# Zeros for the query tiles in eight pieces behind the gates, and two later times in the scheduler of a two-layer hybrid decoder trunk

## The chip, the cores and the metric

The kernel runs on one core of one Trainium2 chip. The metric is the device time of one execution in microseconds (us), as the median of a few runs. One execution was also recorded by the hardware profiler; its rows are given in microseconds from the start of its span. TensorE is called PE here, VectorE DVE, ScalarE ACT, GpSimd POOL, and SyncE, which issues the DMAs, SP.

## The reference, cut to what matters

A sequence of 512 tokens with 1024 features passes through two layers. Each layer is a mixer and a feed-forward part:

```
h = rmsnorm(x);  proj = h @ w_in                       # 1024 -> 3592 columns
aq, ak, av = split(silu(causal_dwconv(a_qkv)))         # 4 heads x 128: gated DeltaNet
beta = sigmoid(a_b);  g = -exp(a_log) * softplus(a_a + dt_bias)
o_a = rmsnorm(gated_delta_rule(l2norm(aq), l2norm(ak), av, g, beta)) * silu(a_z)
o_b = dilated_attention(rope(b_q), rope(b_k), b_v)     # 8 heads x 64
x = x + rmsnorm(concat(o_a, o_b) @ w_out)
u = causal_dwconv(rmsnorm(x) @ ffn_up) + bias
x = x + rmsnorm((gelu(u_gate) * u_val) @ ffn_down)     # 2816 wide
```

The delta rule needs, per chunk, the decay between any two tokens, exp of a difference of cumulative sums of `g`. The dilated attention multiplies roped queries and keys of 64 features per head.

## The kernel before, in words

Activations lie with features on the 128 partitions and the 512 tokens along the free axis. A projection adds up products of 128x128 weight pieces with 128x512 activations in PSUM. Single precision is kept by splitting each operand into a high part in fp32r and a remainder: a row of a projection is three matmuls of 512 columns (high by high twice with the two activation parts, and the remainder of the weights once). In the trace it is a pair of lines, `psg<-hx,whi` x2 and `psg<-hx,wlo` x1. Weights arrive in units of 128x1024 (`raw`, line 250, from SP). ACT writes the high part `whi` (helper `act`, line 147), and DVE or POOL subtracts for the remainder `wlo` (helper `tt`, line 151): DVE as one instruction of 128x1024, POOL as four of 128x256. Which of the two takes a unit is decided when the program is built.

That decision, and the order of all instructions on all engines, comes from a small simulator inside the kernel, `_Sched`. Every stage is a generator. It issues some instructions, adds their modelled cost to a clock of its engine (`sc.op`), and yields the time at which it wants to go on; `sc.get` and `sc.put` model a buffer and the time it comes free, `sc.set` and `sc.wait` a flag. The generator with the best priority that is due goes next. So a yielded time does not delay anything on the chip: it only changes which instruction is written ahead of which, and which engine looks least loaded. On the chip each engine runs its list in order and waits for the data.

PSUM has eight banks: four of kind `g` for projections, three of kind `s`, and one of kind `o`. That single `o` bank serves, one after the other, the norm's sums, the gates and the four decay pieces.

The places that matter here, in the order of the mixer's start:

- The set-up of a layer. The four 128x1024 pieces of `x` are written to memory (`xspill`, line 737), and line 754 sets to zero the halves of two query tiles that stay unused: `qz[0]`, which shares the buffer of `bT[0]` and is called `bT` in the trace, and `qz[1]`, called `qz`. Each is one POOL instruction of 64 partitions by 2048. The simulator's clock for POOL does not count them.
- `gates()`: a chain of small DVE and ACT steps from the projected `dn_ab` to `dn_g`, then a matmul on PE into the `o` bank for the cumulative sums (in the trace `pso<-dn_g,cc`), then `dn_gc`, `dn_kds`, `dn_eg`, and the flag `eg`.
- `conv`: each projected head is scaled out of PSUM on DVE (`A<-psg,rs`) and convolved, one first tap on ACT and three on DVE (`kT<-A,vv,kT`, then `vb<-A,vv,vb`), 128 partitions by about 510 columns each.
- `decays()`: for each of four chunks, four matmuls into the `o` bank (`pso<-cc,dn_g`, recorded as x8), then DVE subtracts (`edec<-pso,dn_gc`), which frees the bank, then two ACT steps. I call the four chunks decay 0 to 3.
- `k_head`: PE transposes a key head (`pss<-cc,kT`), DVE forms `dn_dk` and `kd`.
- `inverse()` and `doubles`: from a memory round trip come `cpt` pieces, which PE multiplies in small matmuls of 16 columns (`pss<-cpt,xiT`, `pss<-C,xi`).
- The end of the mixer: attention's output is added into `bT` (`bT<-pso,bT`), gates multiply the delta rule's output (`vb<-vb,dn_rq`, `zt<-zt,vb`), and both are split for the output projection (`hx<-bT`, `hx<-zt`).

The roped queries are written into the used halves of `qz` by ACT, 64 partitions at a time, behind the query projection.

```
ps = yield from pget("o")            # decays(): the one o bank
r = tt(e[:, c], v4(ps), bc(gc[:, c]), ALU.subtract)
pput("o", r)                         # modelled as free when edec is done
```

Of the kernel before, what the change touches and what calls it, by code (L numbers as in the profile page):

```python
# [18 lines left out]
P = 128  # L19
# [5 lines left out]
NC = S // P  # L25
AH = 8
DH = 64
# [86 lines left out]
def kernel(ctx: ExitStack, tc: tile.TileContext, xT, w_ab, w_cm, w_tm, w_o, w_up, w_dn,  # L114
                      vec, rowc, cst, lnm, out):
    nc = tc.nc
# [12 lines left out]
    sc = _Sched()  # L129
# [20 lines left out]
    def tt(out_, a, b, op, after=0.0, eng="dve"):  # L150
        (nc.vector if eng == "dve" else nc.gpsimd).tensor_tensor(out_, a, b, op=op)  # L151
        n = out_.free_size()
        return sc.op(eng, 0.07 + n * 1.05e-3 if eng == "dve" else 0.18 + n * 2.07e-3, after)
# [18 lines left out]
    def vcopy(out_, a, after=0.0):  # L172
        nc.vector.tensor_copy(out_, a)
        return sc.op("dve", 0.07 + out_.free_size() * 1.0e-3, after)
# [12 lines left out]
    def wget(tag, cols=512):  # L187
        yield from sc.get(tag, BUFS[tag])
        return work(tag, cols)
# [4 lines left out]
    def pget(tag):  # L194
        yield from sc.get("ps" + tag, PB[tag])
        return psum(tag)

    def pput(tag, at):
        sc.put("ps" + tag, at)
# [4 lines left out]
    def bc(ap, n=P):  # L204
        return ap.unsqueeze(2).to_broadcast(list(ap.shape) + [n])
# [504 lines left out]
    def mixer(l, key, hx, acc2, rs, segs):  # L710
# [28 lines left out]
        def small(name, cols=4):  # L739
            return kp.tile([P, 4, cols], F32, tag="dn_" + name, bufs=1, name="dn_" + name)  # L740
# [9 lines left out]
        bT = [sp.tile([P, 4, S], F32, tag=f"s{8 + i}", name=f"bT{i}") for i in range(2)]  # L750
        bv = sp.tile([P, 4, S], F32, tag="s10", name="bv")
        qz = [bT[0], sp.tile([P, 4, S], F32, tag="qz", name="qz")]
        for i in range(2):
            nc.gpsimd.memset(qz[i][DH * (1 - i):DH * (2 - i)], 0.0)
        beta, g, t1, t2, t3, gc, eg, kds, dc, beg, rq, dk, br2, vsc = (small(x) for x in (
            "beta", "g", "t1", "t2", "t3", "gc", "eg", "kds", "dc", "beg", "rq", "dk", "br2", "vsc"))
        ea = kp.tile([P, 4], F32, tag="dn_ea", bufs=1, name="dn_ea")
# [3 lines left out]
        def K(*a):  # L761
            return (l,) + a
# [3 lines left out]
        def gates():  # L766
            ps = yield from pget("o")
            abr = yield from wget("C")
            r = vcopy(abr[0:16], pab[0:16])
            pput("g", r)  # L770
            yield r
            for c in range(NC):
                sc.t += 0.1
                pe.transpose(ps[:, c * 16:(c + 1) * 16], abr[0:16, c * P:(c + 1) * P], ident[0:16, 0:16])
            pv = ps[:, 0:64].rearrange("p (c k) -> p c k", c=4)
            vcopy(ab, pv[:, :, 8:16])
            r = tt(ab, pv[:, :, 0:8], ab, ALU.add)
            pput("o", r)
            sc.put("C", r)
            yield from sc.wait(*ready)  # L780
            r = tt(ab, ab, bc(rt, 8), ALU.mult)
            b, a = ab[:, :, 0:4], ab[:, :, 4:8]
            tables(T_EXP)
            act(ea, rc[:, 0:4], AF.Exp)
            rb = act(beta, b, AF.Exp, scale=-1.0, after=r)
            tt(g, a, rc[:, 4:8].unsqueeze(1).to_broadcast([P, 4, 4]), ALU.add)
            r = stt(t1, g, -1.0, g, ALU.mult, ALU.min)
            r = act(t1, t1, AF.Exp, after=r)
            yield r
            ts(beta, beta, 1.0, None, ALU.add, after=rb)  # L790
            recip(beta, beta)
            ts(t2, t1, 2.0, None, ALU.add)
            recip(t2, t2)
            tt(t1, t1, t2, ALU.mult)
            tt(t2, t1, t1, ALU.mult)
            r = ts(t3, t2, 1.0 / 15, None, ALU.mult)
            for k in (13, 11, 9, 7, 5, 3):
                r = stt(t3, t3, 1.0 / k, t2, ALU.add, ALU.mult, after=r)
            stt(t3, t3, 1.0, t1, ALU.add, ALU.mult)
            ts(g, g, 0.0, None, ALU.max)  # L800
            stt(g, t3, 2.0, g, ALU.mult, ALU.add)
            r = stt(g, g, -1.0, ea.unsqueeze(1).to_broadcast([P, 4, 4]), ALU.mult, ALU.mult)
            yield r + 2.0
            ps = yield from pget("o")
            gf = g.rearrange("p a b -> p (a b)")
            mm(ps[:, 0:16], utri, gf, True, True)
            mm(ps[:, 16:32], one.to_broadcast([P, P]), gf, True, True)
            yield sc.t + 0.15
            last = ps[:, 16:32].rearrange("p (a b) -> p a b", a=4)
            act(dc, last, AF.Exp)  # L810
            vcopy(gc, ps[:, 0:16].rearrange("p (a b) -> p a b", a=4))
            r = tt(kds, last, gc, ALU.subtract)
            pput("o", r)
            yield r
            act(kds, kds, AF.Exp)
            r = act(eg, gc, AF.Exp, after=r)
            sc.set(K("eg"), r)

        def decays():
            for c in range(NC):  # L820
                ps = yield from pget("o")
                for h in range(NH):
                    mm(ps[:, h * P:(h + 1) * P], g[:, c, h:h + 1].to_broadcast([P, P]), utri, True, True)
                yield sc.t + 0.15
                r = tt(e[:, c], v4(ps), bc(gc[:, c]), ALU.subtract)
                pput("o", r)
                yield r
                act(e[:, c], e[:, c], AF.Abs)
                r = act(e[:, c], e[:, c], AF.Exp, scale=-1.0)
                yield  # L830
            sc.set(K("gates"), r)
# [363 lines left out]
        def rope(i, c, ps):  # L1195
            yield from sc.wait(*ready)
            t = yield from wget("AB"[c // 2])
            r = act(t, ps, AF.Identity, scale=rt[:, c:c + 1])
            pput("g", r)
            yield r  # L1200
            sq = yield from sc.get("sq", 2)
            rab = kp.tile([P, 2, AH, 16], F32, tag="sq", bufs=2, name="rab")
            ra, rb = rab[:, 0], rab[:, 1]
            tv = t.rearrange("p (h d) -> p h d", h=AH)

            def tab(tb, lo, hi):
                return tb[:, c, lo:hi].unsqueeze(1).to_broadcast([P, AH, hi - lo])

            tt(ra, tv[:, :, 0:16], tab(cosr, 0, 16), ALU.mult)
            tt(rb[:, :, 0:8], tv[:, :, 8:16], tab(sinr, 0, 8), ALU.mult)  # L1210
            tt(rb[:, :, 8:16], tv[:, :, 0:8], tab(sinr, 8, 16), ALU.mult)
            r = tt(tv[:, :, 0:16], ra, rb, ALU.add)
            sc.put("sq", r)
            yield r
            pt = yield from pget("s")
            transposes(pt, [t[:, p * P:(p + 1) * P] for p in range(4)])
            sc.put("AB"[c // 2], sc.t)
            if i == 0:

                for j in range(2):  # L1220
                    bs = slice(DH * j, DH * (j + 1))
                    r = act(qz[j][bs, :, c * P:(c + 1) * P], v4(pt)[bs], AF.Copy, scale=DH ** -0.5)
            else:
                r = act(bT[i][:, :, c * P:(c + 1) * P], v4(pt), AF.Copy)
            pput("s", r)
            sc.set(K("b", i, c), r)
# [380 lines left out]
```

## Time and profile before

| what | value |
| --- | --- |
| median of 3 runs | 1411.35 us (1409.8 to 1412.21) |
| the profiled execution's own time | 1409.27 us |
| its span, first to last instruction | 1407.5 us |
| mean granted clock of PE in it | 0.989 |
| PE busy | 1365.3 us, 97% of the span, 7176 matmuls and transposes |
| DVE busy | 863.5 us, 61% |
| POOL busy | 706.7 us, 50% |
| ACT busy | 617.6 us, 44% |
| DMA | 123.18 MB, mean 88 GB/s |

The span is 1.77 us shorter than the execution's time, and that time is 2.08 us below the median of the three runs. A timeline line gives start, duration, engine, source line, operation, output and inputs with the tile's size, the number of instructions joined in the line, and in square brackets how long the engine was idle before it and what ended that. Durations of joined lines are from the first start to the last end. A line of windows gives, for a stretch, its length, then the busy time and count of PE, of PE's weight loads, of DVE, ACT and POOL, then the granted clock of PE (1.00 is full), the busy share of the DMA engines and GB/s.

### The profile page before, as it was taken

The page shows a single profiled execution, that of the slowest core. Times are in us where ns is not written, and L with a number is a line of the kernel's source. Part 1 is how long each engine was busy: PE and PEld are TensorE (multiplying, and loading weights), DVE is VectorE, ACT ScalarE, POOL GpSimd, SP SyncE. Part 2 cuts the span into 40 slices and gives each one's busy share as a digit, 9 for nine tenths or more (in the row PEclk, how much of TensorE's full clock was granted, in tenths as well). Part 3 has the DMA queues.
Part 4 walks back from the last instruction along what each step waited for, and adds up shares of the span by engine and source line. Part 5 has one row for each costly group of instructions (what it writes and reads, how often), then busy time and mean ns, then how long its engine had stood idle before and what let it go on. Part 6 is the DMA issues. An engine that isn't in the chain of part 4 may idle for free. (4 is left out here: it accounts for less than half of the span.)

```text
span 1407.5 us, 19286 instructions
## 1 busy us (share of the span) xinstructions
PE 1365.3 (97%) x7176; PEld 1138.0 (81%) x7176; DVE 863.5 (61%) x1520; ACT 617.6 (44%) x998; POOL 706.7 (50%) x767
## 2 busy tenths in 40 slices
PE   9999999998999999999999999999989999999996
PEld 6878777887888888888887877788888888888886
DVE  5774477848677777521469635777568777773213
ACT  5553467535544444232245434665345444433220
POOL 1455266414577777424264642653156777772441
PEclk9999999999999999999999999999999999999998
DMA  5233111042232333233332330112413332323331
GB/s 201 75 94 88 61 46 45 16 158 82 61 104 90 105 91 104 83 109 97 102 117 75 109 89 31 61 31 70 141 46 90 91 104 90 104 87 97 100 92 61
DMA packets 48846, 123.18 MB, mean 88 GB/s; under 512 B 15600, under 2 KB 18416, under 8 KB 48752
## 3 DMA queue, kind: packets, MB, share of 16 engines
q1 hardware_dynamic: 48752, 121.95, 28.3%
q8 instruction: 57, 0.93, 0.3%
q14 instruction: 37, 0.30, 0.1%
HBM read 115.11 MB, written 6.82 MB: 87 GB/s over the span
## 5 line engine op out<-in xcount | busy, mean ns | idle before, releaser
L151 POOL TENSOR_TENSOR wlo<-raw,whi 128x256 fp32r<-128x256 f32 x556 | 497.1, 925 | 357.5 <-ACT whi L147 345.4
L138 PE MATMUL psg<-hx,whi 128*128 128x512 f32 (+1 forms) x2080 | 631.8, 387 | 2.4 <-DVE hx L151 2.4
L138 PEld LDWEIGHTS psg<-hx,whi 128*128 128x128 f32 x2080 | 379.7, 189 | 76.3 <-DVE hx L151 3.0
L147 ACT ACTIVATE whi<-raw 128x1024 fp32r<-128x1024 f32 (+1 forms) x200 | 209.0, 1045 | 429.4 <-PE psg L138 368.5
L138 PE MATMUL psg<-hx,wlo 128*128 128x512 f32 (+1 forms) x1040 | 396.4, 381 | 0.0
L138 PEld LDWEIGHTS psg<-hx,wlo 128*128 128x128 f32 x1040 | 196.3, 189 | 37.6
L165 DVE SCALAR_TENSOR_TENSOR B<-A,vv,B 128x510 f32<-128x510 f32 (+1 forms) x176 | 198.8, 1131 | 39.5 <-ACT B L147 36.2
L138 PE MATMUL psg<-hid,whi 128*128 128x512 f32 (+1 forms) x744 | 213.4, 371 | 0.0
L138 PEld LDWEIGHTS psg<-hid,whi 128*128 128x128 f32 x744 | 135.6, 188 | 24.1
L151 DVE TENSOR_TENSOR wlo<-raw,whi 128x1024 fp32r<-128x1024 f32 (+1 forms) x59 | 74.6, 1267 | 131.0 <-ACT whi L147 130.8
L138 PE MATMUL psg<-hid,wlo 128*128 128x512 f32 (+1 forms) x372 | 137.9, 371 | 0.0
L138 PE MATMUL psg<-whi,hx 128*128 128x512 f32 x384 | 123.0, 401 | 0.6 <-DVE A L151 0.6
L151 POOL TENSOR_TENSOR acc<-acc,sq 128x256 f32<-128x256 f32 (+1 forms) x58 | 56.2, 970 | 92.4 <-ACT sq L147 90.7
L151 DVE TENSOR_TENSOR A<-psg,rs 128x512 f32<-128x512 f32 x100 | 68.7, 689 | 40.8 <-PE psg L138 38.8
L138 PEld LDWEIGHTS psg<-whi,hx 128*128 128x128 f32 x384 | 69.3, 189 | 14.4 <-DVE A L151 1.5
L138 PEld LDWEIGHTS psg<-hid,wlo 128*128 128x128 f32 x372 | 70.0, 188 | 12.0
L138 PE MATMUL psg<-wlo,hx 128*128 128x512 f32 x192 | 75.4, 393 | 0.0
L147 ACT ACTIVATE B<-A,vv 128x512 f32<-128x512 f32 x88 | 70.2, 802 | 2.7 <-DVE A L151 2.6
L147 ACT ACTIVATE C<-B 128x512 f32<-128x512 f32 x44 | 27.7, 631 | 85.9 <-DVE B L165 85.9
L151 DVE TENSOR_TENSOR hid<-C,hid 128x512 fp32r<-128x512 f32 x44 | 36.3, 825 | 28.4 <-ACT hid L147 28.4
L158 POOL TENSOR_SCALAR B<-B,den 128x512 f32<-128x512 f32 (+1 forms) x30 | 41.0, 1369 | 23.8 <-DVE den L177 13.7
L138 PE MATMUL pss<-hx,whome 128*128 128x256 f32 x288 | 42.1, 301 | 5.6 <-DVE hx L165 4.9
(239 smaller groups left out, 1692.4 us busy)
## 6 DMA issues: line engine op xcount, KB each, us to landing
raw<-in_w_up_dram SPq DMA_DIRECT2D x88, 512.0 KB, 3.5
raw<-in_w_cm_dram SPq DMA_DIRECT2D x32, 512.0 KB, 3.6
raw<-in_w_dn_dram SPq DMA_DIRECT2D x32, 512.0 KB, 3.5
raw<-in_w_tm_dram SPq DMA_DIRECT2D x24, 512.0 KB, 3.6
raw<-in_w_o_dram SPq DMA_DIRECT2D x16, 512.0 KB, 3.6
raw<-in_w_dn_dram SPq DMA_DIRECT2D x16, 384.0 KB, 3.1
xt<-in_xT_dram SPq DMA_DIRECT2D x6, 512.0 KB, 6.6
scr_a<-am SPq DMA_DIRECT2D x8, 256.0 KB, 2.6
```

Source lines behind the costliest of these rows:

```text
L138: pe.matmul(ps, lhsT, rhs, start=start, stop=stop)
L147: nc.scalar.activation(out_, in_, func, **kw)
L151: (nc.vector if eng == "dve" else nc.gpsimd).tensor_tensor(out_, a, b, op=op)
L158: e.tensor_scalar(out_, a, s1, None, op0=op0)
L165: nc.vector.scalar_tensor_tensor(out_, a, s, b, op0=op0, op1=op1)
```

## The change

Four edits. The two memsets of the set-up go. In `gates()`, after the flag `eg`, each of the four chunks of tokens gets its zeros by two POOL instructions of 64x512, which POOL's modelled clock counts at 0.45 us each, with at least 1 us of modelled time between chunks; a flag `zero` follows, and the first stage that writes the queries waits for it. The modelled time between the last step of `dn_g` and the matmul that sums it grows from 2 to 4 us. The modelled time at which a decay's bank is free grows by 0.7 us. The arithmetic is the same.

```diff
         qz = [bT[0], sp.tile([P, 4, S], F32, tag="qz", name="qz")]
-        for i in range(2):
-            nc.gpsimd.memset(qz[i][DH * (1 - i):DH * (2 - i)], 0.0)
...
             r = stt(g, g, -1.0, ea.unsqueeze(1).to_broadcast([P, 4, 4]), ALU.mult, ALU.mult)
-            yield r + 2.0
+            yield r + 4.0
             ps = yield from pget("o")
...
             sc.set(K("eg"), r)
+            for c in range(NC):
+                for i in range(2):
+                    nc.gpsimd.memset(qz[i][DH * (1 - i):DH * (2 - i), :, c * P:(c + 1) * P], 0.0)
+                    sc.op("pool", 0.45)
+                yield sc.t + 1.0
+            sc.set(K("zero"))
...
                 r = tt(e[:, c], v4(ps), bc(gc[:, c]), ALU.subtract)
-                pput("o", r)
+                pput("o", r + 0.7)
...
             if i == 0:
+                yield from sc.wait(K("zero"))
                 for j in range(2):
```

The simulator writes other lists of instructions from this. Three places show it. The numbers at the ends of names (as in `bT_6356`) only tell one tile from another of the same kind.

POOL at the entry of layer 1, before, from the last sums of the norm (`acc`) to the first power for the keys (`dn_dk`):

```order
L151 TENSOR_TENSOR acc_5849<-acc_5849,sq 128x256 x5
L754 MEMSET bT_6356 64x2048
L754 MEMSET qz 64x2048
L151 TENSOR_TENSOR acc_5849<-acc_5849,sq 128x256
L372 TENSOR_TENSOR rt<-rt,mhalf 128x2
L151 TENSOR_TENSOR wlo<-raw,whi 128x256 x24
L888 TENSOR_TENSOR dn_dk<-dn_dk,mhalf 128x16
```

and now:

```order
L151 TENSOR_TENSOR acc_5852<-acc_5852,sq 128x256 x6
L372 TENSOR_TENSOR rt<-rt,mhalf 128x2
L151 TENSOR_TENSOR wlo<-raw,whi 128x256 x8
L818 MEMSET bT_6359 64x4x128
L818 MEMSET qz 64x4x128
L151 TENSOR_TENSOR wlo<-raw,whi 128x256 x4
L818 MEMSET bT_6359 64x4x128
L818 MEMSET qz 64x4x128
L818 MEMSET bT_6359 64x4x128
L818 MEMSET qz 64x4x128
```

The large memsets no longer stand among the sums; the eight small ones stand among the weight remainders, and of the six units (x24) that POOL took there four are left (x8, x4, and another x4 behind the last memsets), so that two units have gone to DVE.

DVE at decays 0 to 2 of layer 1, before:

```order
L151 TENSOR_TENSOR A<-psg,rs 128x512 x2
L151 TENSOR_TENSOR edec<-pso,dn_gc 128x512 x2
L165 SCALAR_TENSOR_TENSOR vb<-A,vv,vb 128x509
L165 SCALAR_TENSOR_TENSOR vb<-A,vv,vb 128x510
L165 SCALAR_TENSOR_TENSOR vb<-A,vv,vb 128x511
L165 SCALAR_TENSOR_TENSOR vb<-A,vv,vb 128x509
L165 SCALAR_TENSOR_TENSOR vb<-A,vv,vb 128x510
L165 SCALAR_TENSOR_TENSOR vb<-A,vv,vb 128x511
L151 TENSOR_TENSOR edec<-pso,dn_gc 128x512
L169 TENSOR_REDUCE dn_dk<-sq 128x4
L158 TENSOR_SCALAR dn_dk<-dn_dk 128x4
L151 TENSOR_TENSOR kd<-pss,dn_kds 128x512
```

and now:

```order
L151 TENSOR_TENSOR A<-psg,rs 128x512 x2
L151 TENSOR_TENSOR wlo<-raw,whi 128x1024
L151 TENSOR_TENSOR edec<-pso,dn_gc 128x512 x2
L165 SCALAR_TENSOR_TENSOR vb<-A,vv,vb 128x509
L165 SCALAR_TENSOR_TENSOR vb<-A,vv,vb 128x510
L165 SCALAR_TENSOR_TENSOR vb<-A,vv,vb 128x511
L165 SCALAR_TENSOR_TENSOR vb<-A,vv,vb 128x509
L165 SCALAR_TENSOR_TENSOR vb<-A,vv,vb 128x510
L165 SCALAR_TENSOR_TENSOR vb<-A,vv,vb 128x511
L169 TENSOR_REDUCE dn_dk<-sq 128x4
L158 TENSOR_SCALAR dn_dk<-dn_dk 128x4
L151 TENSOR_TENSOR kd<-pss,dn_kds 128x512
```

One unit's remainder now stands on DVE between the heads' scaling and the first `edec`, and the first key's `dn_dk` and `kd` have passed the third `edec`. On PE, in the same place of layer 1, the matmul on `dn_g` comes four rows of the projection later, decay 0 at the same place, decay 1 two rows later, and decay 2 follows the first twelve transposes after one more row.

DVE at the end of layer 1's mixer, before (`zt<-psg,rs` here is the scaling of the last gate head):

```order
L151 TENSOR_TENSOR zt<-psg,rs 128x512
L151 TENSOR_TENSOR hx_8754<-bT_6356,hx_8754 128x512
L151 TENSOR_TENSOR hx_8753<-zt,hx_8753 128x512
L151 TENSOR_TENSOR hx_8754<-bT_6356,hx_8754 128x512 x2
L151 TENSOR_TENSOR hx_8753<-zt,hx_8753 128x512
L151 TENSOR_TENSOR bT_6356<-pso,bT_6356 64x512
```

and now:

```order
L151 TENSOR_TENSOR zt<-psg,rs 128x512
L151 TENSOR_TENSOR vb<-vb,dn_rq 128x4x128
L151 TENSOR_TENSOR wlo<-raw,whi 128x1024
L151 TENSOR_TENSOR hx_8753<-bT_6359,hx_8753 128x512 x4
L151 TENSOR_TENSOR zt<-zt,vb 128x512 x4
L151 TENSOR_TENSOR hx_8752<-zt,hx_8752 128x512 x4
```

The attention half now comes first in the output projection, with a weight remainder ahead of it, and the last `vb<-vb,dn_rq` stands behind the last gate head's scaling.

## The prediction

> **What bounds the kernel now.** I read the shares first. PE is busy nearly all the time, so only what makes PE wait, or lowers its clock, can move the time.
>
> ```profile
> PE 1365.3 (97%) x7176; PEld 1138.0 (81%) x7176; DVE 863.5 (61%) x1520; ACT 617.6 (44%) x998; POOL 706.7 (50%) x767
> ```
>
> 1407.5 less 1365.3 leaves 42.2 us without a matmul, in two layers. The change adds and removes no matmul, so it can only take from these, from slow-clock stretches, or add to them. Next I looked at PE's waits at the start of layer 1's mixer, where the memsets, gates and decays stand, from 720 to 775 us (waited for, total, times, longest).
>
> ```profile
> PE pso L138 <- DVE dn_g L165: 1.7, 1, 1.7
> PE pso L138 <- POOL acc L151: 1.2, 1, 1.2
> ```
>
> These two are what the change can aim at: 1.71 us for the gates' chain and 1.24 us for POOL's last sum. PE's and POOL's timelines show each.
>
> ```profile
> 725.53 1.81 POOL L754 MEMSET bT<- 64x2048 f32 x1
> 727.39 1.81 POOL L754 MEMSET qz<- 64x2048 f32 x1
> 729.16 0.72 POOL L151 TENSOR_TENSOR acc<-acc,sq 128x256 f32<-128x256 f32 x1
> ...
> 729.93 0.61 PE L138 MATMUL pso<-cc,acc 128*128 128x1 f32 x4 [1.24 <-POOL acc L151]
> 736.43 0.62 PE L138 MATMUL psg<-hx,whi 128*128 128x512 f32 x2
> 737.11 0.62 PE L138 MATMUL psg<-hx,whi 128*128 128x512 f32 x2
> 743.06 0.59 PE L138 MATMUL pso<-dn_g,cc 128*128 128x16 f32 x4 [1.71 <-DVE dn_g L165]
> 756.74 1.16 PE L138 MATMUL pso<-cc,dn_g 128*128 128x128 f32 x8 [0.48 <-DVE edec L151]
> 768.61 0.72 PE L138 MATMUL psg<-whi,hx 128*128 128x512 f32 x2 [0.33 <-DVE A L151]
> ```
>
> The sum that PE waits for stands behind both memsets; without them it could start 3.6 us earlier, so that wait goes. The same stretch in both layers, from the mixer's start to the projection row behind decay 3, shows the difference between them: 44.07 us in layer 1, 42.10 in layer 0, with full clock in both.
>
> ```profile
> 31.99:74.09 42.10, 40.45 (x211) 33.47 (x209) 31.42 (x62) 22.37 (x34) 20.55 (x25) 1.00 0.23 67
> 724.54:768.61 44.07, 39.97 (x205) 32.46 (x203) 33.56 (x63) 22.33 (x35) 22.08 (x26) 1.00 0.38 132
> ```
>
> **Memsets.** In layer 0 they start at 16.6 and 18.5 us, in idle time of POOL (its wait ahead of them is 15.8 us, for data), so nothing is won there. In layer 1 the wait of 1.24 us goes. What does PE meet next? The gates' chain, and it does not start earlier: on ACT, `dn_beta` stands behind a `whi` whose weights land late.
>
> ```profile
> SPq L1091 <- DMA xspill<-xt: 5.4, 1, 5.4
> ...
> 731.08 0.38 SPq L250 DMA_DIRECT2D raw<-in_w_cm_dram  x1
> ...
> 734.78 1.06 ACT L147 ACTIVATE whi<-raw 128x1024 fp32r<-128x1024 f32 x1 [1.20 <-DMA raw<-in_w_cm_dram]
> 735.84 0.20 ACT L147 ACTIVATE dn_beta<-dn_ab 128x16 f32<-128x16 f32 x1
> ```
>
> SP issues that load at 731.08, behind the load of `xw`, which waits 5.4 us for the spill of `x`. No POOL work is in this. SP's list and ACT's are the same there in the changed program. So `dn_g` is ready where it was, at 742.9, and PE's 1.24 us would only lengthen the second wait to 2.95, did the second edit not move that matmul.
>
> **Two microseconds more for the gates.** The matmul on `dn_g` comes four rows later. A row is three matmuls, 0.69 us (736.43 to 737.11 from one start to the next, at full clock). PE arrives at 743.06 - 1.71 - 1.24 + 4 x 0.69 = 742.87, and waits some 0.2 us. So PE is 1.24 + 1.71 - 0.2 = 2.75 us ahead. If that lasted, it would be the gain.
>
> **Decays: where it goes.** Behind `dn_g` the pace is DVE's, and its list is full without a gap up to decay 0's `edec`:
>
> ```profile
> 742.74 0.18 DVE L165 SCALAR_TENSOR_TENSOR dn_g<-dn_g,dn_ea 128x16 f32<-128x16 f32 x1
> 742.83 4.55 DVE L165 SCALAR_TENSOR_TENSOR kT<-A,vv,kT 128x509 f32<-128x509 f32 x6
> 748.79 6.10 DVE L165 SCALAR_TENSOR_TENSOR kT<-A,vv,kT 128x509 f32<-128x509 f32 x6
> 754.81 1.28 DVE L151 TENSOR_TENSOR A<-psg,rs 128x512 f32<-128x512 f32 x2
> 756.01 0.68 DVE L151 TENSOR_TENSOR edec<-pso,dn_gc 128x512 f32<-128x512 f32 x1
> 758.97 4.55 DVE L165 SCALAR_TENSOR_TENSOR vb<-A,vv,vb 128x509 f32<-128x509 f32 x6 [0.34 <-ACT vb L147]
> 764.04 0.68 DVE L169 TENSOR_REDUCE dn_dk<-sq 128x4 f32<-128x512 f32 x1
> 765.29 0.68 DVE L151 TENSOR_TENSOR kd<-pss,dn_kds 128x512 f32<-128x512 f32 x1
> ...
> L151 DVE TENSOR_TENSOR wlo<-raw,whi 128x1024 fp32r<-128x1024 f32 (+1 forms) x59 | 74.6, 1267 | 131.0 <-ACT whi L147 130.8
> ...
> 749.77 7.79 POOL L151 TENSOR_TENSOR wlo<-raw,whi 128x256 fp32r<-128x256 f32 x8 [7.39 <-ACT whi L147]
> ...
> 726.74 1.23 DVE L151 TENSOR_TENSOR wlo<-raw,whi 128x1024 fp32r<-128x1024 f32 x1 [2.10 <-ACT whi L147]
> ```
>
> The order now puts one weight remainder of 1.23 us on DVE between `A` and the first `edec`. The six convolutions beside POOL's `wlo` took 6.10 us against 4.55 beside an idle POOL; the changed order has one unit of `wlo` less there, and I take 0.3 of the 1.55 back (bounds 0 and 1.55). Then decay 0's `edec` ends at 756.69 + 1.2 - 0.3 = 757.6. There is one `o` bank, so decay 1 cannot start before. PE would be there at 756.26 (where it arrived) - 2.75 + 2 rows x 0.69 = 754.9, and waits 2.7 us. The lead is spent at this place.
>
> Behind it, DVE: the second `edec` to 759.4, six convolutions 4.5 to 763.9, the first key's `dn_dk` pair and `kd` (1.95 from 764.04 to 765.97 before) to 765.8. The four transposes of the last key wait for a bank that this `kd` frees, now ahead of decay 3, so PE idles again some 2 us there unless it is late anyhow. Then the third `edec`, the next `kd`, two `A` to 768.9; I place the row that stood at 768.61 at 769.8. **Layer 1's front: +1.2.** Bounds: -2.75 if the lead lasts (DVE is not the limit); +2.7 if the idle time also brings a slow-clock stretch that nothing hides, 1.53 us as at the inverse below.
>
> The Trainium skill ("SBUF — State Buffer", SBUF: two separate sides) has DVE and GpSimd share a port pair by an exclusive lock, in which the loser stops for the whole instruction. By it six convolutions beside 7.8 us of POOL would have been held for most of that, not for 1.55 us; the trace disagrees in size. The page also limits the lock on two-input DVE operations to GpSimd operations that read SBUF, and the 1.23 us remainder that ran wholly beside the old memsets, against a mean of 1.27, agrees.
>
> **Layer 0.** The same edits put decay 1 and the first twelve transposes one row later, and one remainder on DVE. There DVE sits idle 1.31 us ahead of the second `edec`:
>
> ```profile
> 63.50 0.69 DVE L151 TENSOR_TENSOR edec<-pso,dn_gc 128x512 f32<-128x512 f32 x1 [1.31 <-PE pso L138]
> ```
>
> That idle time covers the 1.23; the third decay's wait grows or shrinks by tenths. I take +0.3 (0 to +1.3, the whole remainder).
>
> **The inverse's first small matmuls.** Layer 1 waits 0.39 us for `cpt` and then runs at a lower clock; layer 0 does neither. The order now has a row more ahead of `cpt` and another between its two groups.
>
> ```profile
> 142.17 1.10 PE L138 MATMUL pss<-cpt,xiT 128*64 128x16 f32 x16
> 152.28 0.27 PE L138 MATMUL pss<-sq,xi 64*64 64x64 f32 x1
> ...
> 837.13 1.08 PE L138 MATMUL pss<-cpt,xiT 128*64 128x16 f32 x16 [0.39 <-DMA cpt<-scr_xt]
> 848.77 0.27 PE L138 MATMUL pss<-sq,xi 64*64 64x64 f32 x1
> ...
> 840.00:843.00 3.00, 3.00 (x13) 2.35 (x13) 0.70 (x2) 1.70 (x4) 2.35 (x4) 0.62 0.05 19
> ```
>
> From first to last of these rows: 10.11 us in layer 0, 11.64 in layer 1; the clock costs 1.53. With full rows in between, the stretch of 16-column matmuls is shorter, as in layer 0. I take both away: **-1.9** (bounds -1.9 and +1.1, the latter if a drop comes in layer 0 too, 1.53, and only the wait goes).
>
> The Trainium skill ("TensorE: Matmul & The Clock Gate", Part 1) gives a free-running window of about 3.4 us, and lets the clock fall after an idle one. By it a stall of 1.7 or 2.7 us would cost no clock, and the front's upper bound would be +1.2 too. The trace has the fall with PE listed as busy throughout, on thin matmuls, so partial use is enough.
>
> **The end of layer 1's mixer.**
>
> ```profile
> 970.92 0.39 PE L138 MATMUL pso<-pt1l,vh 128*128 128x256 f32 x1 [0.27 <-DVE pt1l L151]
> 973.42 0.50 PE L138 MATMUL psg<-hx,whi 128*128 128x512 f32 x1 [1.19 <-DVE hx L151]
> ...
> 970.78 0.68 DVE L151 TENSOR_TENSOR zt<-psg,rs 128x512 f32<-128x512 f32 x1
> 971.55 0.69 DVE L151 TENSOR_TENSOR hx<-bT,hx 128x512 fp32r<-128x512 f32 x1
> ...
> 972.00:976.00 4.00, 2.81 (x8) 2.03 (x8) 3.97 (x6) 3.75 (x7) 1.96 (x2) 0.73 0.24 58
> ```
>
> PE now waits 0.27 + 1.19 = 1.46 us, and a slow stretch follows. In the new order the last `vb<-vb,dn_rq` stands behind the last gate head's `zt` (0.68), which needs PE's last projection row; PE's four transposes of `vb` follow, and wait for both: 0.68 + 0.68 and about 0.1 of handing over, 1.45. The first `hx<-bT` then stands behind a remainder of 1.23 that DVE starts after `vb`: 1.23 + 0.69, of which four transposes and the first high matmul cover some 0.8 by my estimate (one row's time and a little), so PE waits 1.1 more. **+1.1** (2.55 against 1.46). Bounds: -2.6 if attention's earlier finish takes both the waits and the slow clock (0.27 of 4 us, 1.1); +2.5 if the first rows each wait for a split.
>
> Attention's middle keeps its order but for starting about two rows earlier: 0, with 1.5 either way, what one slow stretch costs at the inverse.
>
> **Sum.** 1.2 + 0.3 - 1.9 + 1.1 = +0.7. Against the profiled execution's 1409.27 that is 1410.0. The median of the runs is 2.08 above that execution, so 1412.1 is the predicted median, no change that can be measured: the runs tell 0.2%, 2.8 us.
>
> **Rivals.**
>
> *The lead lasts* (faster). Layer 0 passes the same stretch in 42.10 us, 1.97 less. If ACT and DVE catch up in layer 1 as there, the front gives -2.75, the inverse -1.9, the end 0 to +1.1: about -4, 1407.4. Against it: the chain DMA, `whi`, `dn_beta`, `dn_g`, in which DVE is full, starts no earlier.
>
> *DVE becomes the bound* (slower). Four units of remainders move from POOL to DVE, 4.9 us of DVE work. Place: the first `edec` of each layer, and the split of `hx`. If all its 1.23 in layer 0 (+1.3), the front's +2.7 and the end's +2.5 come, less the 1.9: +4.6, 1416.0. It decides once DVE's idle time ahead of the second `edec` is under 1.23 us, and the stall at decay 1 brings the slow clock.
>
> *The slow clock only wanders.* By what the trace shows, a drop follows thin stretches, and shifts of a microsecond or two move which ones. With a drop less at the end too (-1.1) the time is 1411.0; with one kept at the inverse, 1413.6. Both still unmeasurable.
>
> *The edit's waits cost elsewhere.* The flag for the zeros could hold the queries: in layer 0 and 1 the memsets end before the query heads, so 0.
>
> **Chances.** Forecast and the wandering clock 0.48; the lead lasts 0.25; DVE the bound 0.27. So faster by over 0.2% 0.23, within it 0.47, slower 0.30. The range runs from the first rival to the second, 1407.4 to 1416.0; the likeliest case's own range is 1410.5 to 1414.
>
> **What would show it.** Right: no wait for `acc`, a wait for `dn_g` below 0.5, a wait for `edec` of 2 to 3 us ahead of decay 1 of layer 1, DVE's list there without gaps, no low clock behind `cpt`, and at the mixer's end 2 to 3 us of waits for `vb` and `hx`. Wrong: no stall at decay 1 with `edec` on time (the lead lasts), or low clock right behind decay 1 and a row behind decay 3 at over 771 us (the slow side).

## The result, and the profile after

| | before | changed |
| --- | --- | --- |
| median of 4 runs each | 1410.57 us (1407.23 to 1412.21) | 1423.99 us (1422.78 to 1427.95) |
| profiled execution: span | 1407.5 us | 1422.1 us |
| mean granted clock of PE | 0.989 | 0.986 |

The ratio is 1.0103, with a 95% interval of 1.0073 to 1.0132: slower by some 14 us, above the whole range that was predicted (1407.4 to 1416.0). Executions that took over 100 us longer than the others of their kernel are left out of every ratio and every profile below.

The shares of the changed kernel's page:

```profile
PE 1370.7 (96%) x7176; PEld 1142.2 (80%) x7176; DVE 862.3 (61%) x1525; ACT 620.3 (44%) x1002; POOL 684.0 (48%) x755
```

1422.1 less 1370.7 leaves 51.4 us without a matmul, 9.2 more than before; the other 5.4 are in PE's busy time, which grows though the matmuls are the same 7176. So nearly two thirds are waits. The rest is mostly matmuls at a lower clock: the table below has 10.2 us more at half clock, which is worth at most 5.1. Both traces have the same number of matmuls, so I took the start of each k-th one in both and looked at how far they are apart. The rows' order differs, so this is sharp only at places that all rows of a stage have passed; four such places in layer 1 serve as marks below. For each stage: how much longer it is than in the profiled execution of before, and in brackets the time PE spent at half clock in it.

```
                      to 718 us  entry,gates,decays  inverse     attention,end   rest    sum
                      of before     718 - 792        792 - 849     849 - 993
before (half clock)                    (0)             (3.4)          (3.4)
changed                 +0.78      +4.20 (3.4)      +5.27 (10.2)   +3.86 (3.4)   +0.45  +14.56
```

The waits of PE after the norm of layer 1, from the entry to the keys, in the changed kernel. `acc` is gone from the list, `dn_g` is down, and `edec` is what PE waits for now:

```profile
744.15 0.59 PE L138 MATMUL pso<-dn_g,cc 128*128 128x16 f32 x4 [0.79 <-DVE dn_g L165]
760.18 2.07 PE L138 MATMUL pso<-cc,dn_g 128*128 128x128 f32 x8 [4.17 <-DVE edec L151]
769.90 0.63 PE L143 MATMUL pss<-cc,kT 128*128 128x128 f32 x4 [1.50 <-DVE kd L151]
772.39 0.73 PE L138 MATMUL psg<-whi,hx 128*128 128x512 f32 x2 [0.83 <-DVE A L151]
```

The stall was forecast at this place, with 2.7 us; it is 4.17. The row behind decay 3 stands at 772.39, 3.78 later than before (0.78 of it from ahead of 718). DVE's timeline shows what the forecast did not have, a gap ahead of `dn_gc` (first line before, then the changed kernel):

```profile
747.90 0.17 DVE L173 COPY dn_gc<-pso 128x16 f32<-128x16 f32 x1
...
749.00 0.68 DVE L151 TENSOR_TENSOR A<-psg,rs 128x512 f32<-128x512 f32 x1
750.89 0.17 DVE L173 COPY dn_gc<-pso 128x16 f32<-128x16 f32 x1 [1.21 <-ACT dn_dc L147]
751.19 6.01 DVE L165 SCALAR_TENSOR_TENSOR kT<-A,vv,kT 128x509 f32<-128x509 f32 x6
758.31 1.21 DVE L151 TENSOR_TENSOR wlo<-raw,whi 128x1024 fp32r<-128x1024 f32 x1
759.44 0.68 DVE L151 TENSOR_TENSOR edec<-pso,dn_gc 128x512 f32<-128x512 f32 x1
```

and ACT's, why `dn_dc` came then: it now stands behind a `kT`, which waits for DVE, and a `whi` (first line before).

```profile
743.69 0.18 ACT L147 ACTIVATE dn_dc<-pso 128x16 f32<-128x16 f32 x1 [4.18 <-PE pso L138]
...
749.11 0.72 ACT L147 ACTIVATE kT<-A,vv 128x512 f32<-128x512 f32 x1 [9.92 <-DVE A L151]
749.75 1.04 ACT L147 ACTIVATE whi<-raw 128x1024 fp32r<-128x1024 f32 x1
750.69 0.16 ACT L147 ACTIVATE dn_dc<-pso 128x16 f32<-128x16 f32 x1
```

At the inverse, where 1.9 us were to be won, PE waits 2.35 us in the middle of the small matmuls (first line before, where the same group waits for nothing):

```profile
838.14 1.95 PE L138 MATMUL pss<-C,xi 64*128 64x16 f32 x16
...
841.74 1.10 PE L138 MATMUL pss<-cpt,xiT 128*64 128x16 f32 x16
846.09 3.56 PE L138 MATMUL pss<-C,xi 64*128 64x16 f32 x16 [2.35 <-DVE C L173]
...
844.59 1.23 DVE L151 TENSOR_TENSOR wlo<-raw,whi 128x1024 fp32r<-128x1024 f32 x1 [5.31 <-ACT whi L147]
845.73 0.21 DVE L173 COPY C<-pss 64x64 f32<-64x64 f32 x1
...
843.50 1.06 ACT L147 ACTIVATE whi<-raw 128x1024 fp32r<-128x1024 f32 x1 [8.16 <-DMA raw<-in_w_cm_dram]
```

DVE sat idle for 5.31 us. The small copy `C` stood in its list behind a weight remainder, which waited for ACT's high part, and that for a DMA. The copy's input was ready at about 842.8. Before, the same unit of weights was POOL's. The windows of 3.4 us show what followed:

```profile
841.60:845.00 3.40, 2.13 (x20) 1.49 (x19) 0.41 (x1) 1.50 (x2) 0.00 (x0) 1.00 0.72 281
845.00:848.40 3.40, 2.31 (x11) 2.34 (x12) 1.78 (x7) 0.71 (x2) 0.00 (x0) 0.50 0.46 131
848.40:851.80 3.40, 3.40 (x13) 2.80 (x14) 1.03 (x3) 0.00 (x0) 0.00 (x0) 0.50 0.06 23
851.80:855.20 3.40, 3.40 (x19) 2.51 (x18) 0.00 (x0) 1.44 (x3) 0.00 (x0) 0.50 0.00 0
855.20:858.60 3.40, 3.40 (x40) 2.78 (x38) 2.31 (x10) 0.35 (x1) 0.00 (x0) 0.99 0.00 0
```

Three windows in a row ran at half clock, where before there was one.

The waits of PE from there to the end of the mixer (778 to 1000 us):

```profile
PE pss L138 <- DVE C L173: 2.4, 1, 2.4
PE psg L138 <- DVE nm L1267: 1.6, 4, 0.8
PE pss L143 <- DVE vb L151: 1.5, 1, 1.5
PE psg L143 <- POOL B L158: 1.4, 2, 1.2
PE psg L138 <- DVE pt1l L151: 1.4, 1, 1.4
PE psg L138 <- DVE hx L151: 0.8, 1, 0.8
...
```

and the same list before (775 to 985 us):

```profile
PE psg L138 <- DVE hx L151: 1.2, 1, 1.2
PE pss L143 <- DVE A L151: 0.9, 2, 0.5
PE psg L138 <- DVE nm L1262: 0.9, 1, 0.9
PE psg L138 <- DVE pt1l L151: 0.4, 2, 0.2
PE pss L138 <- DMA cpt<-scr_xt: 0.4, 1, 0.4
...
```

In attention `pt1l`, `B` and `nm` are longer, and at the end `vb` is new. The end itself came as forecast: 1.47 for `vb` (1.45) and 0.79 for `hx` (1.1).

### The profile page after: what moved, and what is told of

Same layout as the page of the kernel before. It is cut to its first block, busy times and chain, and to the rows that moved or that the text cites. A ratio compares the mean times of both kernels' runs of the same rounds, so it can differ in the third digit from the quotient of the medians.

```text
span 1422.1 us, 19277 instructions
## 1 busy us (share of the span) xinstructions
PE 1370.7 (96%) x7176; PEld 1142.2 (80%) x7176; DVE 862.3 (61%) x1525; ACT 620.3 (44%) x1002; POOL 684.0 (48%) x755
## 5 line engine op out<-in xcount | busy, mean ns | idle before, releaser
L151 POOL TENSOR_TENSOR wlo<-raw,whi 128x256 fp32r<-128x256 f32 x536 | 478.0, 922 | 399.1 <-ACT whi L147 382.7
L151 DVE TENSOR_TENSOR wlo<-raw,whi 128x1024 fp32r<-128x1024 f32 (+1 forms) x64 | 80.4, 1259 | 139.5 <-ACT whi L147 139.4
L158 POOL TENSOR_SCALAR B<-B,den 128x256 f32<-128x256 f32 (+1 forms) x28 | 36.8, 1316 | 27.4 <-DVE den L177 20.4
```

The source lines that it names most:

```text
L158: e.tensor_scalar(out_, a, s1, None, op0=op0)
```

## The experiments

The first question was whether the edits cost time at their own places, or whether the loss comes with the other lists of instructions that the simulator wrote. The lists themselves tell where to cut. The edits are three in what follows: the zeros (the old memsets go and the small ones come), the gates' 4 us, and the later bank. I counted the instructions that differ from before, over five engines, one that moves counting at its old place and at its new one. Counted zeros and the gates' 4 us together make 104 differences; counted zeros and the later bank together make 1621, nearly as many as all three, 1675. If only the memsets' cost on POOL's modelled clock is left out, all three edits make 104.

**All edits, memsets not counted**

```diff
             for c in range(NC):
                 for i in range(2):
                     nc.gpsimd.memset(qz[i][DH * (1 - i):DH * (2 - i), :, c * P:(c + 1) * P], 0.0)
-                    sc.op("pool", 0.45)
-                yield sc.t + 1.0
```

> All three edits of the change, but the eight small memsets are not counted on POOL's modelled clock and no modelled time passes between them. The lists of all engines then stay those of before but for some twenty rows, and no unit of weight remainders changes its engine. Theory A (the loss comes with the new plan that the counted memsets set off, not with what the edits do at their own places): 1407 to 1413 us, no wait for the norm's sum, and PE's wait for dn_g longer or decay 1 later by what was won, low clock as before. Theory B (the loss comes from the edits at their places, above all the later bank and the later dn_g): 1418 us or more.

Measured: 1411.84 us median, ratio to before 1.0028 (1.0011 to 1.0044). Theory A, though not quite no change: the interval leaves 2 to 6 us.

**Zeros and bank, without the gates' edit**

```diff
-            yield r + 4.0
+            yield r + 2.0
             ps = yield from pget("o")
```

> The counted zeros and the later bank, without the two microseconds more for the gates. The lists are those of the changed kernel but for some 23 rows: six units of remainders on DVE as there. Theory A: as slow as the changed kernel, 1420 to 1427 us. Theory B: some of the loss goes with the gates' edit, under 1420.

Measured: 1424.67 us, ratio 1.0125 (1.0106 to 1.0143), as slow as the changed kernel. Its waits from 718 to 800 us are others, with no wait for `edec` at all:

```profile
PE pso L138 <- DVE dn_g L165: 3.4, 1, 3.4
PE pss L143 <- DVE kd L151: 1.6, 1, 1.6
...
```

and still the stage is +2.64, with a half-clock window of 3.4 us in it. So here PE's lead is spent as well, on another wait.

**One decision of the planner fixed**

```diff
+            eng = {114: "pool"}.get(u, eng)
             step = cols if eng == "dve" else 256
```

Units are counted through the program; 114 is the third of the four of attention's query projection in layer 1. Its remainder is the one that stands ahead of decay 0's `edec` in the changed kernel.

> The changed kernel with one decision of the planner fixed: the unit of weight remainders that it gives to DVE between the heads' scaling and decay 0's edec in layer 1 goes to POOL, on the chip and in the modelled clocks. With that alone the lists of layer 1 fall back to those of before but for some 30 rows; all three edits and the counted memsets stay. Theory A (the loss is that of the new plan, and this one decision sets it off): 1408 to 1413 us, within 0.3% of before, waits in the inverse and in attention as before. Theory B (the edits at their places cost): 1418 or more.

Measured: 1410.93 us, ratio 1.0007 (0.9986 to 1.0028). All three edits are in this kernel, and the counted memsets too. With one unit's engine decided as before, the plan of layer 1 falls back to the old one, and the loss is gone. So some 1% hangs on a choice between two engines that the memsets' modelled 3.6 us and the bank's 0.7 tipped: neither of the two alone brings the new plan.

**The six units back on POOL, in the new plan**

Six units of weights had changed from POOL to DVE: one in layer 0, five in layer 1. Here they are written by POOL again, but their modelled cost stays on DVE, so that no other row moves.

```diff
-                r = tt(lo[:, cs], raw[:, cs], hi[:, cs].bitcast(F32), ALU.subtract, eng=eng)
+                (nc.vector if real == "dve" else nc.gpsimd).tensor_tensor(
+                    lo[:, cs], raw[:, cs], hi[:, cs].bitcast(F32), op=ALU.subtract)
...
+                r = sc.op(eng, 0.07 + n * 1.05e-3 if eng == "dve" else 0.18 + n * 2.07e-3)
```

with `real` taken from a table of units.

> The changed kernel with all six units of weight remainders that had gone from POOL to DVE written by POOL again, at the same places of the program; every other row stays. Theory C, widened to all stalls (DVE's added 7 us are the loss): 1410 to 1413. If the moved units cost only at decay 0's edec (1.2 us) and at the inverse (4.9), and attention's loss of 4.5 us is due to the order of rows: 1416 to 1419. Theory D: 1422 or more.

Measured: 1417.05 us, ratio 1.0065 (1.0039 to 1.0091), in the middle case that was written down. The units carry some 5 to 7 us of the loss, not all. The profiled execution is the fastest of the four (1412.86 us), with no half clock between 718 and 993 us.

**Only the unit ahead of the inverse back on POOL**

The same edit for unit 126 alone, the third of the delta rule's query projection; its two runs:

> The changed kernel with one unit of weight remainders (the third of layer 1's query projection, whose subtraction stands on DVE ahead of the first copies of the inverse's small products) written by POOL as before; its modelled cost stays on DVE, so every other row of every list stays. Theory C (this one subtraction, which waits for ACT's high part and so for a late DMA, holds the copies, and the idle time brings three slow-clock stretches): the wait of 2.4 us for C goes and the low clock behind it, 4 to 5 us less than the changed kernel, about 1419. Theory D (the rows' order on PE leaves too little cover there, whoever subtracts): no more than 1 us less, 1423 to 1424.

> Once more the changed kernel with the third unit of layer 1's query projection subtracted by POOL, for a profile at full clock. Theory C: PE's wait of 2.4 us for C is gone, and at most one slow-clock stretch is left behind the first small matmuls of the inverse; the rest as in the changed kernel; 4 to 5 us less than it, about 1419. Theory D: a wait of over 1.5 us stays there.

Measured: ratio 1.0086 (1.0057 to 1.0115) the first time, in four executions that lie in two pairs (1415.60 and 1416.26, 1422.87 and 1423.58), and 1415.42 us, ratio 1.0051 (1.0031 to 1.0071), in ten executions the second time, which is more than the 4 to 5 us that were expected. The second has the profile. The waits from 778 to 1000 us have no `C` any more, and attention's are as they were:

```profile
PE psg L138 <- DVE nm L1273: 1.6, 4, 0.8
PE pss L143 <- DVE vb L151: 1.5, 1, 1.5
PE psg L143 <- POOL B L158: 1.4, 2, 1.2
PE psg L138 <- DVE pt1l L151: 1.4, 1, 1.4
...
```

and DVE's copy follows PE's group at once, with POOL's remainder out of its way:

```profile
841.03 0.22 DVE L173 COPY C<-pss 64x64 f32<-64x64 f32 x1 [3.06 <-PE pss L138]
...
843.42 3.17 POOL L295 TENSOR_TENSOR wlo<-raw,whi 128x256 fp32r<-128x256 f32 x4 [4.52 <-PE pss L138]
```

No half clock is left in the inverse, and that stage is -1.26 against before where the changed kernel had +5.27: 6.5 us for one instruction of 1.23 us on the other engine, some 1.5 of them the half-clock window that before has there too. It does not rest on one pair of profiles. With the new plan and the unit on DVE, the stage is +5.27 in the changed kernel, +4.63 with zeros and bank and +4.67 with the late taps below, and PE waits 2.4, 2.9 and 2.8 us for `C`. With the new plan and the unit on POOL it is -1.26, -0.29 with the six units, and +0.27 with the scaling on ACT below, and no wait for `C` is there. That is 4.4 to 6.5 us. Theory C holds. The -1.26 is what the prediction expected of the inverse once nothing stalls it (-1.9), less a part.

**Attention: taps behind the split**

```diff
-                r = conv_rest(y, u, taps, r)
+                late.append(taps_now)          # query heads of layer 1; modelled cost as before
...
+                if qp == 1 and late:           # behind the next split pt1l
+                    late.pop(0)()
```

> The changed kernel with the three DVE taps of each query head of layer 1 written behind the next split of attention's weights (pt1l) rather than ahead of it; their modelled cost stays where it was, so all other rows stay. Theory E (in attention the new order puts 2.3 us of taps ahead of the split that frees PE's bank): the wait of 1.4 us for pt1l goes, with the slow-clock stretch behind it, 2 to 3 us less than the changed kernel, about 1421. Rival: the wait moves to the next thing in the chain (the scaling of B on POOL, 1.4 us already), and the time stays within 1 us.

Measured: 1426.73 us, ratio 1.0131 (1.0098 to 1.0163). Theory E falls, and its rival did not say enough: the stage of attention and end grew to +8.20, 4.3 more than in the changed kernel, of which one more half-clock window can be 1.7. The waits moved and got longer (890 to 1000 us):

```profile
PE psg L138 <- DVE nm L1280: 3.0, 3, 2.1
PE pso L138 <- DVE pt1l L151: 3.0, 3, 2.4
...
```

**Attention: scaling on ACT** (with unit 126 on POOL)

```diff
-                    r = ts(s_[:, :n], s_[:, :n], den, None, ALU.mult, eng="pool")
+                    nc.scalar.activation(s_[:, :n], s_[:, :n], AF.Copy, scale=den)   # layer 1
+                    r = sc.op("pool", 0.17 + n * 8.5e-4)
```

> The changed kernel with the inverse's unit on POOL as above and, in layer 1's attention, every scaling by den that POOL did done by ACT at the same place; its modelled cost stays on POOL, so all other rows stay. Theory G (attention's loss of 4.6 us against before is POOL's slow scaling, 2.1 us for 512 columns): the wait for B (1.4) goes and attention is 2 to 4 us shorter. Rival (the order in which PE's rows and attention's parts alternate is the loss): the waits move to other parts and attention stays within 1 us.

Measured: 1421.95 us, ratio 1.0095 (1.0064 to 1.0126). Theory G falls: `B` is waited for 0.7 instead of 1.4, but `A` is now late on ACT, and attention is longer by 3.4 us (+5.76 against +2.33 with unit 126 alone), of which a half-clock window can be 1.7. Its rival, within 1 us, does not fit either.

```profile
PE psg L143 <- ACT A L1291: 3.1, 2, 2.7
...
PE psg L143 <- ACT B L1291: 0.7, 1, 0.7
```

So of attention it is shown that the loss goes with the new plan. Where the stage has no half clock, it is -1.20 to -1.28 in the four kernels of the table below with the old plan and +2.28 to +2.33 in the three with the new one: 3.5 us, of which the end's longer waits are 0.8. It is also shown that moving either of two single engines' work does not take it away. Which of the new plan's rows there does is left open.

**The front, edit by edit.** Each edit alone keeps the old plan.

> The kernel before with the gates' 4 us alone: the sum of dn_g stands four rows later on PE, dn_dc on ACT behind a kT and a whi, two copies on DVE behind one A; nothing else moves. Theory F (the edit's own place costs, because the bank's first reader is now late on ACT): PE's wait for dn_g goes (1.7), but dn_gc on DVE waits some 1.2 us for dn_dc and all behind it is late; the stretch of layer 1 from the norm's sums to the keys' transposes (718 to 792 us before) 0 to 1.5 us longer, a wait for edec of over 2 us ahead of decay 1. Rival (the later bank is what costs): that stretch 1 us or more shorter.

> The kernel before with the later decay bank alone: decay 1 and the twelve transposes one or two rows later on PE, nothing else moves. Theory F: the waits for edec (1.1 in both layers) go, the stretch from 718 to 792 us within 0.5 us of before. Rival: 1 us or more longer.

> The kernel before with the zeros in eight uncounted pieces behind the gates, and nothing else moved on any other engine. If the gates are anchored by the weights' load (as the prediction held): the wait for acc (1.24) goes and the one for dn_g grows from 1.7 to 2.9; the stretch from 718 to 792 us within 0.4 us of before. If POOL's memsets held the gates back: dn_g waits 1.7 or less, 1.2 us or more shorter.

Measured: gates' 4 us alone 1411.73 us, ratio 1.0017 (0.9996 to 1.0038); later bank alone 1409.47, 1.0002 (0.9988 to 1.0017); zeros alone, uncounted, 1414.6, 1.0030 (1.0008 to 1.0053). The stages, as above:

```
                      to 718   718 - 792     792 - 849    849 - 993    rest     sum
gates' 4 us alone     +0.14   +2.30 (3.4)  +1.37 (3.4)  -0.01 (3.4)   +0.39   +4.19
later bank alone      +0.12   +1.03 (3.4)  +0.54 (3.4)  -1.26 (0)     +2.00   +2.43
zeros, uncounted      +4.49   +1.18 (3.4)  +0.44 (3.4)  -1.20 (0)     +0.41   +5.32
all three, uncounted  +1.40   +2.38 (3.4)  -2.02 (0)    -1.28 (0)     +1.18   +1.66
unit 114 on POOL      -0.91   +2.33 (6.8)  +0.29 (3.4)  -1.20 (0)     +1.14   +1.65
zeros and bank        +2.02   +2.64 (3.4)  +4.63 (6.8)  +2.32 (0)     +0.87  +12.48
six units on POOL     -1.61   +2.79 (0)    -0.29 (0)    +2.28 (0)     +0.39   +3.56
unit 126 on POOL      +0.28   +3.31 (3.4)  -1.26 (0)    +2.33 (0)     +0.52   +5.18
```

The zeros alone: `acc` is no longer waited for, `dn_g` is waited for longer, and the stage is no shorter. It is +1.18, where within 0.4 was expected, with a half-clock window in it.

```profile
PE pso L138 <- DVE dn_g L165: 3.6, 1, 3.6
...
```

The sum of the two waits before was 2.95. So the memsets were not what held the gates, as predicted. Of this profile's 5.32 us, 4.49 lie ahead of 718 us, with two half-clock windows more than before; why this kernel's median is 0.3% up is not shown. The gates' 4 us alone take the wait for `dn_g` away and put 4.3 us for `edec` in its place; the gap of 1.21 us ahead of `dn_gc` is there, and theory F said where from. Its size was missed (2.30 against 0 to 1.5), and a half-clock window of 3.4 us is in it. The later bank alone was to be within 0.5 and is +1.03, with such a window too; how much of the one is the edit I can't tell from one profile.

**Which reader of the bank comes first**

```diff
-            act(dc, last, AF.Exp)
             vcopy(gc, ps[:, 0:16].rearrange("p (a b) -> p a b", a=4))
             r = tt(kds, last, gc, ALU.subtract)
+            act(dc, last, AF.Exp)
```

> The kernel with the gates' 4 us alone, and the copy dn_gc and the difference dn_kds written ahead of ACT's dn_dc, which reads the same bank; no row of any list moves, only which of the readers comes first. Theory F (dn_gc waits 1.2 us on DVE because dn_dc, ahead of it on the bank, stands behind a kT and a whi on ACT): the wait goes, the second six taps, the heads' scaling and decay 0's edec come 1.2 us earlier, and the stretch from 718 to 792 us is 1 to 2 us shorter than with the 4 us alone (2.3 over before there), or more where the slow clock at decay 1 goes too. Rival (dn_gc waits for something else that came at the same time): no change in dn_gc's start.

Measured: 1410.25 us, ratio 1.0008 (0.9984 to 1.0032); the stage is +0.57 where it was +2.30, and DVE's copy follows `A` without a gap, though ACT's `dn_dc` is as late as ever:

```profile
749.16 0.68 DVE L151 TENSOR_TENSOR A<-psg,rs 128x512 f32<-128x512 f32 x1
749.76 0.16 DVE L173 COPY dn_gc<-pso 128x16 f32<-128x16 f32 x1
...
750.86 0.17 ACT L147 ACTIVATE dn_dc<-pso 128x16 f32<-128x16 f32 x1
```

Theory F holds in the stage, though the medians of the two kernels are too close to tell apart. Two engines that only read the same bank waited for each other in the order in which the program wrote them. In the built lists this wait is a semaphore: `dn_gc` waits for ACT's counter when it stands second and for PE's when it stands first, and then `dn_dc` waits for DVE's.

**The anchor**

```diff
-        sync.dma_start(lm, lnm)
...
             sc.set(K("eg"), r)
+            sync.dma_start(lm, lnm)
```

on top of the uncounted zeros (first run), and with the gates' 4 us and `dn_gc` first as well (second run).

> The kernel before with two things moved and no list changed beside them: the zeros in eight uncounted pieces behind the gates, and SP's load of the mask table (xw) behind the gates too, so that it no longer holds back the weights that follow it. If the gates' chain is anchored by that load, as the prediction held: the weights land 4 to 5 us earlier, dn_beta follows rs and comes 2.4 us earlier, the waits for acc (1.24) and most of the one for dn_g (1.71) go, and decay 0's edec follows: 2.4 us less in layer 1's front than before, 1406 to 1407 beside 1408.6. If the anchor is another (POOL, or the DVE chain itself): dn_g waits 2.9 and the time is that of before.

> The kernel before with uncounted zeros behind the gates, the mask's load behind the gates, the gates' 4 us, and dn_gc ahead of dn_dc. The three waits of the front (acc 1.24, dn_g 1.71, dn_gc) are then all gone; what is left is decay 1's wait for edec. If the two measured pieces add: the stretch from 718 to 792 us 2.5 to 3.5 us shorter than before, 1405.5 to 1407 beside 1409. If DVE's chain to decay 0 is the limit alone: no shorter than with zeros and the mask's load moved (2.85).

Measured: 1408.98 us, ratio 0.9999 (0.9980 to 1.0018), and 1405.43 us, ratio 0.9969 (0.9947 to 0.9991). In the first the stage from 718 to 792 us is 2.85 shorter than before, in the second 3.00, and of the front's waits the largest that is left in the second is:

```profile
PE pso L138 <- DVE edec L151: 0.9, 1, 0.9
...
```

SP's queue in the second kernel shows the weights' load at 724.03, right behind the spill, where it stood at 731.08 before:

```profile
720.29 3.64 SPq L737 DMA_DIRECT2D xspill<-xt  x4
724.03 1.10 SPq L250 DMA_DIRECT2D raw<-in_w_cm_dram  x1
```

So the anchor that the prediction named is the right one, and with it moved the front's gain is real. The second kernel is faster than the one before, by 0.3%; the first one's 2.85 us in the profile do not show in its median, within an interval of 2.7 us either way. The two cases written down for the second kernel are not told apart by 3.00 against 2.85, and that its median is lower for its two further edits and not by chance is not shown.

## Why the prediction was wrong

The terms of the sum that failed are the front's (+1.2, measured +4.20), the inverse's (-1.9, measured +5.27) and attention's (0).

- **Memsets and anchor: right.** "The gates' chain ... does not start earlier", since `dn_beta` stands behind a `whi` whose weights land late. Zeros alone: the wait moves from `acc` to `dn_g` (3.6 us, forecast 2.95). The load moved: 2.85 us won.
- **The matmul on `dn_g`: right in kind.** 0.2 us of wait forecast, 0.79 measured, over the 0.5 that was named as a sign.
- **Decays: the mechanism right, the size wrong.** The lead is spent at decay 1, as said, with 4.17 us instead of 2.7. The step that failed is "Behind `dn_g` the pace is DVE's, and its list is full without a gap". I had compared ACT's list up to `dn_beta`, where it is the same, and not four rows further, where `dn_dc` had moved behind a `kT` and a `whi`. That gap is 1.21 us. Of the 0.3 us of relief for the convolutions 0.1 came (6.01 us). (The first key's steps, taken as 1.95 us, are 1.93 by their rows; it changes nothing.) And the stall emptied a whole window:

```profile
756.30:759.70 3.40, 0.00 (x0) 0.00 (x0) 3.37 (x6) 2.40 (x2) 2.02 (x4) 1.00 0.39 146
759.70:763.10 3.40, 2.92 (x13) 2.92 (x14) 1.23 (x3) 3.28 (x5) 0.00 (x0) 0.50 0.49 154
```

  The front is +4.20 against +1.2 forecast, and above the bound of +2.7, which had the half clock in it but not the gap.
- **Layer 0: right.** The difference is +0.78 us at 60 us, +1.23 at 74, behind the decays (0.45 for a forecast of 0.3), and again +0.78 at 718. The first 0.78 is there by 20 us.
- **The inverse: wrong in sign, the largest miss.** "With full rows in between, the stretch of 16-column matmuls is shorter ... I take both away: -1.9". The rows on PE were read, DVE's list at that place was not. It has a weight remainder ahead of the first copies:

```
L151 TENSOR_TENSOR xi<-cpt,cc 64x512 x2
L151 TENSOR_TENSOR wlo<-raw,whi 128x1024
L173 COPY C<-pss 64x64
L158 TENSOR_SCALAR C<-cpt,cc 128x4x16
```

  It was counted among the units that had gone to DVE, at 1.23 us each, and its cost was put at places where DVE looked full. Its price is not its duration but what it waits for, and that it lets a chain of small steps wait with it. Taken back, the stage is 4.4 to 6.5 us shorter.
- **Attention's middle: wrong.** "Keeps its order but for starting about two rows earlier: 0, with 1.5 either way." Attention and the end together are +3.86, of which the end was forecast with +1.1. The waits grew in `pt1l`, `B` and `nm`; the new plan brings it, the row that does was not found, so this step's cause stays open.
- **The end: right in its waits**, 2.26 against 2.55, and the half-clock window that stood there before is gone; one stands in attention's middle instead, at 913 us.
- **The rival "DVE becomes the bound"** had the right sign and the right kind of cause (remainders that move from POOL to DVE) and the wrong places, "the first `edec` of each layer, and the split of `hx`", so that its price, 4.6 us, was a third of what came. It counted four units; six moved, 7.4 us at 1.23 each. The rival "the lead lasts" is refuted by every kernel that keeps the load where it was.
- **The slow clock.** The Trainium skill ("TensorE: Matmul & The Clock Gate", Part 1) lets the clock fall after an idle window of about 3.4 us. The window from 756.3 to 759.7 had no matmul, and the next ran at 0.50: there the trace agrees. The one from 841.6 to 845.0 was busy for 2.13 us of 3.40 and the clock fell behind it as well, and it stayed low through two windows that were listed as busy throughout, in which two rows of 512 columns ran among smaller matmuls and transposes. For a bound on a stall's price here, partial use has to count.

## What to carry to other kernels

Where a build-time planner writes the lists, a small edit of its costs is a new program: read every engine's list at every stage whose rows moved, and ask of each row that was put ahead of a short chain what it waits for, not how long it runs. Before taking a wait away, follow the chain behind it to the thing that sets its time (here a load queued behind another load that waited for a spill); a wait taken away in front of it comes back further on. And write the urgent reader of a shared PSUM bank first.

## What the runs showed that was not expected

- Two engines reading one PSUM bank are ordered by the program: `dn_gc` on DVE waited 1.21 us for `dn_dc` on ACT in each of the eight profiled kernels with the gates' 4 us and `dn_dc` first, and not at all in the two where it was written first.
- The choice of one engine for one 1.23 us subtraction made 1582 differences in the five lists (unit 114, counted as above) and some 1% of the time.
- In executions of nearly the same program the half-clock windows lie elsewhere. Ahead of layer 1's places, the start of the 3680th matmul (718 us) lies between 1.6 us earlier and 4.5 later than in the profile of before, and the runs of the kernel before that count lie between 1403.67 and 1419.79 us. The 2.85 us of the moved load show in a stage of the profile with no half clock in it, and not in a median.
